# Weaving the high and low weights of a tile element by element, with activation rows 320 columns apart

## The chip, the cores and the metric

The kernel runs on one core of one Trainium2 chip. The metric is the device time of one execution, in microseconds (us). The kernel before takes 2366.43 us (median of three runs, 2366.19 to 2366.48). One more execution was taken with the hardware profiler; its own time is 2366.29 us, and the instructions in its trace span 2364.5 us of that.

## The reference, cut to what matters

A two-layer encoder on 256 tokens plus 16 meta tokens (272 rows, 256 in the last layer's later steps), width 2048, all in float32:

```python
proj = h @ w_in                       # (272 x 2048) @ (2048 x 6176): both head groups
y_gla = gla_mixer(...)                # bidirectional gated linear attention, 4 heads
y_na = na_mixer(...)                  # 2-D neighbourhood attention, 16 heads
mix = concat([y_gla, y_na]) @ w_out   # (272 x 2048) @ (2048 x 2048)
h = layer_norm(ALPHA * h + mix)
ff = square(relu(h @ w_ff1)) @ w_ff2  # 2048 -> 8192 -> 2048
h = layer_norm(ALPHA * h + ff)
```

Nearly all of the arithmetic is in the four products with `w_in`, `w_out`, `w_ff1` and `w_ff2`.

## The kernel before, in words

**Precision.** TensorE takes the operands as float32r, which keeps fewer bits than float32. So each number is split into a high part (rounded to float32r) and a low part (what the rounding lost), and a product is three matmuls: high weights by high activations, high weights by low activations, low weights by high activations.

**Weights.** They stream from HBM once, in 768 tiles of 128 partitions by 1024 columns (`order`, `weights`, `made`, lines 150 to 184). A tile is eight blocks of 128 x 128. For each, SP issues a DMA into `raw` (L179), ScalarE casts `raw` to `wh` (L180), VectorE subtracts, `wl = raw - wh` (L181). The pool `wst` has three buffers each of `raw`, `wh` and `wl`, so a tile's cast waits until the matmuls with the `wh` of three tiles before are done, and `weights` makes each tile one tile ahead of its use. The first tile is put together in smaller pieces (`head`, L186 to L202).

**Activations.** They lie transposed, 128 features by tokens, as a `Pair` (L43): one tile of `[128, 2, PITCH]` whose two rows are the high and the low part. With `PITCH` = 288 a row starts 1152 bytes behind the one before it. In this program the high rows of the tiles that the four products read start at multiples of 256 bytes in the partition, the low rows 128 bytes past such a multiple, and every block of `wh` and `wl` at a multiple of 512 bytes plus 256. In the last layer, where only 256 tokens are left, some pairs are dense: the low row follows at column 256.

**Products.** `by_m` (L250) makes one output block of 128 features at a time: for every weight tile `eight` (L204) issues its matmuls into one PSUM bank. Where 272 (or 258, 274) columns are wanted these are 16 matmuls with `wh` (L216: each block twice, with the high and the low row) and 8 with `wl` (L219). Where 256 are wanted (`once`) they are 8 matmuls of 512 columns with `wh` (L213: the high and the low row in one instruction) and 8 of 256 columns with `wl` (L219). `by_k` (L230) uses a tile for four outputs at once, 24 matmuls (L246); that is 56 of the 768 tiles, 16 of them with 256 columns. Every matmul loads its own weights: 128 columns of 4 bytes in each partition, read at a step of 4 bytes.

**Around them.** Attention, gates and norms are generators that `pump` steps between the products (queues `fg` and `bg`); `issue_after(self.wl)` puts what they issue behind the latest split of weights. A scheduler orders each engine's instructions by its own estimates. The matmuls of these parts, among them the low-rank gate (L403, loads of 64 and 32 columns) and `gla_head` (L446 to L642), use other tiles than `wh` and `wl`. `merge` (L543) and `gather` (L534) of `gla_head` work on strided rows. `mean` (L876) takes its pair, "sp", from `pair` (L277) too.

The constructor of the program in `kernel` sets a scratch of 8192 bytes in each partition for DMA descriptors.

Of the kernel before, what the change touches and what calls it, by code (L numbers as in the profile page):

```python
# [7 lines left out]
F32 = mybir.dt.float32  # L8
F32R = mybir.dt.float32r
U8 = mybir.dt.uint8  # L10
AF = mybir.ActivationFunctionType
ALU = mybir.AluOpType
PSUM = bass.MemoryType.PSUM

P = 128
# [4 lines left out]
L = T + NM  # L20
# [6 lines left out]
WB = 1024  # L27
# [9 lines left out]
WARM = 14  # L37
MEET = 2
PAD = 40
PITCH = 288  # L40


class Pair(tuple):  # L43
# [10 lines left out]
class Trunk:  # L54
# [117 lines left out]
    def made(self, ap, ends):  # L172
        if ap is None:
            return None
        nc = self.nc
        raw, wh, wl = (self.wp.tile([P, WB], d, name=nm, tag=nm)
                       for nm, d in (("raw", F32), ("wh", F32R), ("wl", F32R)))
        for c in map(slice, (0,) + ends, ends):
            nc.sync.dma_start(raw[:, c], ap[:, c])  # L179
            nc.scalar.copy(wh[:, c], raw[:, c])  # L180
            self.wl = nc.vector.tensor_tensor(wl[:, c], raw[:, c], wh[:, c].bitcast(F32), ALU.subtract).ins  # L181
        if not ends:
            self.head(ap, raw, wh, wl)
        return wh, wl

    def head(self, ap, raw, wh, wl):  # L186

        nc, q = self.nc, WB // 4
        both = self.xr.tile([P, 2, q + L], F32, name="head", tag="head", bufs=1)
        self.x[:2] = [self.pair(self.xp, "x", c) for c in range(2)]  # L190
        for c in range(2):
            nc.sync.dma_start(both[:, c], self.i["head"][:, c])
        nc.sync.dma_start(raw[:, 2 * q:], ap[:, 2 * q:])
        for c in range(2):
            at = slice(c * q, c * q + q)
            h, lo = (t[:, :L] for t in self.x[c])
            todo = [(both[:, c, q:], h, lo), (both[:, c, :q], wh[:, at], wl[:, at])]
            for args in todo[::-1] if c else todo:
                self.split(*args)
        for at in (slice(2 * q, 3 * q), slice(3 * q, WB)):  # L200
            nc.scalar.copy(wh[:, at], raw[:, at])
            self.wl = nc.vector.tensor_tensor(wl[:, at], raw[:, at], wh[:, at].bitcast(F32), ALU.subtract).ins  # L202

    def eight(self, ps, wh, wl, x, n, first, last, once):  # L204

        mm = self.nc.tensor.matmul
        c = lambda w, j: w[:, j * P:j * P + P]  # L210
        for j, v in enumerate(x):
            if once:
                mm(ps, lhsT=c(wh, j), rhs=v.once, start=first and not j, stop=False)  # L213
                continue
            for i in range(2):
                mm(ps[:, :n], lhsT=c(wh, j), rhs=v[i][:, :n], start=first and not i + j, stop=False)  # L216
        o = ps[:, T:] if once else ps[:, :n]
        for j, (h, _) in enumerate(x):
            mm(o, lhsT=c(wl, j), rhs=h[:, :T if once else n], start=False, stop=last and j == 7)  # L219
# [10 lines left out]
    def by_k(self, acts, n, before, wide=False):  # L230

        ps = [self.pm.tile([P, 512], F32, name="mm", tag="mm") for _ in range(4)]
        if wide:
            ps += [self.bank() for _ in range(4)]
        nk = len(acts)
        for k in range(0, nk, 2):
            before(k)
            for g in range(0, len(ps), 4):
                wh, wl = self.weights()
                parts = ((wh, 0), (wh, 1), (wl, 0))  # L240
                order = [(j, p, m) for j in range(2) for p in range(3) for m in range(4)]
                by_output = k == nk - 2 or k == 0 and not wide
                order.sort(key=lambda o: (o[0], o[2] // 2) if wide and not k + g else (by_output and o[2], o[1] // 2))
                for j, p, m in order:
                    c = j * 512 + m * P
                    self.nc.tensor.matmul(ps[g + m][:, :n], lhsT=parts[p][0][:, c:c + P], rhs=acts[k + j][parts[p][1]][:, :n],  # L246
                                          start=k + j + p == 0, stop=k == nk - 2 and j + p == 3)
        return [p[:, :n] for p in ps]

# [25 lines left out]
        self.nc.vector.tensor_tensor(dst[low:low + n], src, dst[high[0]:high[0] + n].bitcast(F32), ALU.subtract)  # L275

    def pair(self, pool, name, c):  # L277
        both = pool.tile([P, 2, PITCH], F32R, name=f"{name}{c}", tag=f"{name}{c}", bufs=1)
        return Pair(both, dense=name in ("y", "u") and not self.full)


# [92 lines left out]
    def load_gates(self):  # L374

        place = lambda c: self.yp.tile([P, 2, PITCH], F32, name=f"gw{c}", tag=f"y{c}", bufs=1).rearrange("p a c -> p (a c)")[:, :512]
        *self.wup, self.wlr = (place(c) for c in (8, 9, 10))
# [563 lines left out]
    def reuse(self, name, c, dtype):  # L941

        t = self.xp.tile([P, 2, PITCH], dtype, name=f"{name}{c}", tag=f"x{c}", bufs=1)
        return t.rearrange("p a c -> p (a c)")[:, :512]
# [235 lines left out]
```

## Time and profile before

| | |
|---|---|
| median of 3 runs | 2366.43 us |
| profiled execution, its own time | 2366.29 us |
| span of its instructions | 2364.5 us |
| granted TensorE clock, mean | 0.999 |
| HBM read | 414.03 MB, 176 GB/s over the span |
| share of 16 DMA engines used by the weights' queue | 55.8% |

How to read it: PE is TensorE's matmuls and PEld its weight loads, which overlap the matmuls; DVE is VectorE, ACT is ScalarE, POOL is GpSimd, SP is SyncE. A group's row gives line, engine, operation, out<-in, shape and count, then busy time, mean duration of one, and the idle time before. A matmul's duration is longer than its pace, since matmuls are pipelined: the mean 272-column matmul lasts 287 ns, but the next one starts about 125 ns after it. The pace is read from the chain of work that ended last, where the time of a piece is the time to the next piece, so that its time over its count is the spacing of its matmuls.

### The profile page before, as it was taken

Reading aid. Unit: us, or ns where it says so; the run is one execution under the profiler, and the core shown is the slowest. Engines: PE = TensorE matmul, PEld = TensorE weight load, DVE = VectorE, ACT = ScalarE, POOL = GpSimd, SP = SyncE. Lnnn points to the kernel's source line nnn. Section 1 sums busy time; section 2 is a strip of 40 time slices with the busy share of each in tenths; the row PEclk is TensorE's granted clock in tenths of the full one; section 3 lists DMA queues with packets and bytes.
Section 4 is the critical chain, followed back from the end, with each engine's and each line's share of the span. In section 5 each row is a group of like instructions: output and inputs, shape, how many; then the busy total and the mean of one; then the engine's idle time right before and its main releaser. Section 6 shows DMA issues by size and latency. Waiting matters only on the chain.

```text
span 2364.5 us, 44607 instructions
## 1 busy us (share of the span) xinstructions
PE 2356.2 (100%) x18180; PEld 2241.9 (95%) x18180; DVE 1520.8 (64%) x2432; ACT 1219.3 (52%) x2100; POOL 136.2 (6%) x200
## 2 busy tenths in 40 slices
PE   9999999999999999999999999999999999999998
PEld 9999999999999999999999899999988888888888
DVE  5588777775544455546576787778766455666654
ACT  5666664564433344444456666655644333444443
POOL 0021100100000000000030111101100000000000
PEclk9999999999999999999999999999999999999999
DMA  7454445555555555555555555455566666556664
GB/s 261 153 160 153 156 135 176 173 176 178 177 178 176 176 177 179 177 177 174 177 184 171 164 160 165 155 160 188 187 192 190 189 187 188 188 190 212 195 188 144
DMA packets 118301, 419.02 MB, mean 177 GB/s; under 512 B 13512, under 2 KB 14024, under 8 KB 118096
## 3 DMA queue, kind: packets, MB, share of 16 engines
q1 hardware_dynamic: 117808, 415.65, 55.8%
q8 instruction: 142, 2.33, 0.4%
q14 instruction: 63, 0.52, 0.1%
q10 hardware_dynamic: 288, 0.52, 0.1%
HBM read 414.03 MB, written 2.10 MB: 176 GB/s over the span
## 4 chain that ended last, share of the span: by engine, by line
PE 98%; DVE 1%; issue 0%; ACT 0%; POOL 0%; DVEq 0%; ACTq 0%; POOLq 0%
PE mm L216 35%; PE mm L219 29%; PE mm L213 22%; PE mm L246 6%; PE bg L246 1%; PE bg L757 1%; PE mm L696 1%; PE bg L557 0%; PE bg L403 0%; DVE wl L181 0%; PE mm L722 0%; PE mm L446 0%; PE bg L883 0%; PE bg L608 0%; PE bg L638 0%
## 5 line engine op out<-in xcount | busy, mean ns | idle before, releaser
L181 DVE TENSOR_TENSOR wl<-raw,wh 128x1024 fp32r<-128x1024 f32 (+1 forms) x768 | 941.8, 1227 | 621.5 <-ACT wh L180 618.4
L180 ACT CAST wh<-raw 128x1024 fp32r<-128x1024 f32 (+1 forms) x768 | 803.5, 1047 | 919.4 <-PE mm L216 367.7
L216 PE MATMUL mm<-x,wh 128*128 128x272 f32 (+2 forms) x4224 | 569.8, 287 | 0.0
L216 PEld LDWEIGHTS mm<-x,wh 128*128 128x128 f32 x4224 | 541.1, 188 | 0.8 <-PE mm L696 0.2
L219 PE MATMUL mm<-x,wl 128*128 128x272 f32 (+3 forms) x3264 | 466.9, 285 | 0.0
L219 PEld LDWEIGHTS mm<-x,wl 128*128 128x128 f32 x3264 | 437.5, 189 | 11.6
L213 PE MATMUL mm<-x,wh 128*128 128x512 f32 x1152 | 290.1, 394 | 0.0
L213 PEld LDWEIGHTS mm<-x,wh 128*128 128x128 f32 x1152 | 207.2, 189 | 37.9 <-PE mm L696 0.4
L219 PE MATMUL mm<-y,wl 128*128 128x272 f32 (+1 forms) x1408 | 200.5, 285 | 0.0
L219 PEld LDWEIGHTS mm<-y,wl 128*128 128x128 f32 x1408 | 189.5, 189 | 6.5
L216 PE MATMUL mm<-y,wh 128*128 128x272 f32 (+1 forms) x1440 | 193.3, 286 | 0.0
L216 PEld LDWEIGHTS mm<-y,wh 128*128 128x128 f32 x1440 | 184.3, 188 | 0.0
L213 PE MATMUL mm<-y,wh 128*128 128x512 f32 x688 | 172.6, 392 | 0.0
L219 PE MATMUL mm<-u,wl 128*128 128x272 f32 (+1 forms) x1024 | 145.8, 285 | 0.0
L213 PEld LDWEIGHTS mm<-y,wh 128*128 128x128 f32 x688 | 123.6, 189 | 21.9
L219 PEld LDWEIGHTS mm<-u,wl 128*128 128x128 f32 x1024 | 137.8, 189 | 4.8
L216 PE MATMUL mm<-u,wh 128*128 128x272 f32 (+1 forms) x1056 | 141.2, 286 | 0.0
L216 PEld LDWEIGHTS mm<-u,wh 128*128 128x128 f32 x1056 | 134.9, 188 | 0.0
L213 PE MATMUL mm<-u,wh 128*128 128x512 f32 x496 | 124.2, 392 | 0.0
L213 PEld LDWEIGHTS mm<-u,wh 128*128 128x128 f32 x496 | 89.2, 189 | 15.9
L246 PE MATMUL mm<-x,wh 128*128 128x272 f32 (+1 forms) x512 | 73.3, 288 | 0.0
L246 PEld LDWEIGHTS mm<-x,wh 128*128 128x128 f32 x512 | 67.9, 191 | 0.0
(273 smaller groups left out, 1856.5 us busy)
## 6 DMA issues: line engine op xcount, KB each, us to landing
raw<-in_wff SPq DMA_DIRECT2D x512, 512.0 KB, 3.6
raw<-in_win SPq DMA_DIRECT2D x190, 512.0 KB, 3.8
raw<-in_wout SPq DMA_DIRECT2D x64, 512.0 KB, 3.6
nb<-in_nab SPq DMA_DIRECT2D x16, 352.0 KB, 4.7
xraw<-in_xT SPq DMA_DIRECT2D x7, 272.0 KB, 5.2
out<-out SPq DMA_DIRECT2D x5, 256.0 KB, 3.2
brow<-in_norm SPq DMA_DIRECT2D x4, 256.0 KB, 4.8
gw<-in_wup SPq DMA_DIRECT2D x4, 196.0 KB
```

Of the source, the lines that this page charges most:

```text
L180: nc.scalar.copy(wh[:, c], raw[:, c])
L181: self.wl = nc.vector.tensor_tensor(wl[:, c], raw[:, c], wh[:, c].bitcast(F32), ALU.subtract).ins
L213: mm(ps, lhsT=c(wh, j), rhs=v.once, start=first and not j, stop=False)
L216: mm(ps[:, :n], lhsT=c(wh, j), rhs=v[i][:, :n], start=first and not i + j, stop=False)
L219: mm(o, lhsT=c(wl, j), rhs=h[:, :T if once else n], start=False, stop=last and j == 7)
L246: self.nc.tensor.matmul(ps[g + m][:, :n], lhsT=parts[p][0][:, c:c + P], rhs=acts[k + j][parts[p][1]][:, :n], start=k + j + p == 0, stop=k ...
L696: nc.tensor.matmul(ps[hh][:, t * NKEY:t * NKEY + NKEY], lhsT=q[hs, NM + t * P:NM + t * P + P], rhs=k[hs, t, :], start=True, stop=True)
L757: nc.tensor.matmul(po[t][hs, :P], lhsT=v2[ts, hs] if rest else v1[:, t, hs], rhs=p2[ts, hh, :] if rest else p1[:, 2 * hh + t, :], start=re ...
```

## The change

The two halves of a weight tile share one tile `w` of 2 x 1024 + 64 columns. High and low weights alternate: high, low, high, low. So one half's 128 columns of a block are read (and written, by the cast and the split) at a step of 8 bytes, and a block of one half covers 1024 bytes instead of 512. `BASE` puts the weave 32 columns (128 bytes) into the tile. In the changed program the high half of every block starts 128 bytes past a multiple of 256, the low half 132. `PITCH` becomes 320, so every row, high or low, of the pairs for the four products starts at a multiple of 256 bytes. The pair "sp" of `mean` gets rows of 272. There are still three buffers, now of `raw` and `w`. The scratch for descriptors becomes 2048 bytes, which makes room for the wider rows. Each engine issues as many instructions as before: the same matmuls with the same columns, casts, splits and DMAs. The scheduler places some of them a little differently; on PE that is a few dozen matmuls.

```diff
-PITCH = 288
+PITCH = 320
+BASE = 32
...
     def made(self, ap, ends):
...
-        raw, wh, wl = (self.wp.tile([P, WB], d, name=nm, tag=nm)
-                       for nm, d in (("raw", F32), ("wh", F32R), ("wl", F32R)))
+        raw = self.wp.tile([P, WB], F32, name="raw", tag="raw")
+        blocks = raw.rearrange("p (b c) -> p b c", c=P)
+        wh, wl = self.woven()
         for c in map(slice, (0,) + ends, ends):
             nc.sync.dma_start(raw[:, c], ap[:, c])
-            nc.scalar.copy(wh[:, c], raw[:, c])
-            self.wl = nc.vector.tensor_tensor(wl[:, c], raw[:, c], wh[:, c].bitcast(F32), ALU.subtract).ins
+            self.halves(blocks, wh, wl, slice(c.start // P, c.stop // P))
...
+    def woven(self):
+        flat = self.wp.tile([P, 2 * WB + 64], F32R, name="w", tag="w")
+        both = flat[:, BASE:BASE + 2 * WB].rearrange("p (b c i) -> p i b c", c=P, i=2)
+        return both[:, 0], both[:, 1]
+
+    def halves(self, raw, wh, wl, at):
+        self.nc.scalar.copy(wh[:, at], raw[:, at])
+        self.wl = self.nc.vector.tensor_tensor(wl[:, at], raw[:, at], wh[:, at].bitcast(F32), ALU.subtract).ins
...
     def eight(self, ps, wh, wl, x, n, first, last, once):
...
-        c = lambda w, j: w[:, j * P:j * P + P]
+        c = lambda w, j: w[:, j]
...
     def by_k(self, acts, n, before, wide=False):
...
-                    c = j * 512 + m * P
-                    self.nc.tensor.matmul(ps[g + m][:, :n], lhsT=parts[p][0][:, c:c + P], rhs=acts[k + j][parts[p][1]][:, :n],
+                    self.nc.tensor.matmul(ps[g + m][:, :n], lhsT=parts[p][0][:, 4 * j + m], rhs=acts[k + j][parts[p][1]][:, :n],
...
     def pair(self, pool, name, c):
-        both = pool.tile([P, 2, PITCH], F32R, name=f"{name}{c}", tag=f"{name}{c}", bufs=1)
+        both = pool.tile([P, 2, L if name == "sp" else PITCH], F32R, name=f"{name}{c}", tag=f"{name}{c}", bufs=1)
...
-    nc = bacc.Bacc("TRN2", target_bir_lowering=False, num_devices=1, dynamic_dma_scratch_size=8192)
+    nc = bacc.Bacc("TRN2", target_bir_lowering=False, num_devices=1, dynamic_dma_scratch_size=2048)
```

`head` is changed in the same way: it splits its pieces by blocks, through `halves`.

More of the change, by code (lines that the diff above doesn't have):

```diff
@@ L175, in made, with head @@
         nc = self.nc
-        raw, wh, wl = (self.wp.tile([P, WB], d, name=nm, tag=nm)
-                       for nm, d in (("raw", F32), ("wh", F32R), ("wl", F32R)))
+        raw = self.wp.tile([P, WB], F32, name="raw", tag="raw")
+        blocks = raw.rearrange("p (b c) -> p b c", c=P)
+        wh, wl = self.woven()
         for c in map(slice, (0,) + ends, ends):
             nc.sync.dma_start(raw[:, c], ap[:, c])
-            nc.scalar.copy(wh[:, c], raw[:, c])
-            self.wl = nc.vector.tensor_tensor(wl[:, c], raw[:, c], wh[:, c].bitcast(F32), ALU.subtract).ins
+            self.halves(blocks, wh, wl, slice(c.start // P, c.stop // P))
         if not ends:
-            self.head(ap, raw, wh, wl)
+            self.head(ap, raw, blocks, wh, wl)
         return wh, wl
-    def head(self, ap, raw, wh, wl):
+    def woven(self):
[5 more added lines that the diff above has]
+        self.wl = self.nc.vector.tensor_tensor(wl[:, at], raw[:, at], wh[:, at].bitcast(F32), ALU.subtract).ins
+    def head(self, ap, raw, blocks, wh, wl):
         nc, q = self.nc, WB // 4
@@ L194, in head @@
         for c in range(2):
-            at = slice(c * q, c * q + q)
+            at = slice(2 * c, 2 * c + 2)
             h, lo = (t[:, :L] for t in self.x[c])
-            todo = [(both[:, c, q:], h, lo), (both[:, c, :q], wh[:, at], wl[:, at])]
+            todo = [(both[:, c, q:], h, lo), (both[:, c, :q].rearrange("p (b c) -> p b c", c=P), wh[:, at], wl[:, at])]
             for args in todo[::-1] if c else todo:
                 self.split(*args)
-        for at in (slice(2 * q, 3 * q), slice(3 * q, WB)):
-            nc.scalar.copy(wh[:, at], raw[:, at])
-            self.wl = nc.vector.tensor_tensor(wl[:, at], raw[:, at], wh[:, at].bitcast(F32), ALU.subtract).ins
+        for at in (slice(4, 6), slice(6, 8)):
+            self.halves(blocks, wh, wl, at)
     def eight(self, ps, wh, wl, x, n, first, last, once):
         mm = self.nc.tensor.matmul
-        c = lambda w, j: w[:, j * P:j * P + P]
+        c = lambda w, j: w[:, j]
         for j, v in enumerate(x):
```

## The prediction

> **What bounds the kernel now.** I read the head of the page first, for the busy shares and the clock, then the chain that ended last.
>
> ```profile
> span 2364.5 us, 44607 instructions
> PE 2356.2 (100%) x18180; PEld 2241.9 (95%) x18180; DVE 1520.8 (64%) x2432; ACT 1219.3 (52%) x2100; POOL 136.2 (6%) x200
> PEclk9999999999999999999999999999999999999999
> ## 4 chain that ended last, share of the span: by engine, by line
> PE 98%; DVE 1%; issue 0%; ACT 0%; POOL 0%; DVEq 0%; ACTq 0%; POOLq 0%
> PE mm L216 35%; PE mm L219 29%; PE mm L213 22%; PE mm L246 6%; PE bg L246 1%; PE bg L757 1%; PE mm L696 1%; PE bg L557 0%; PE bg L403 0%; DVE wl L181 0%; PE mm L722 0%; PE mm L446 0%; PE bg L883 0%; PE bg L608 0%; PE bg L638 0%
> ```
>
> TensorE is never idle, its clock is granted in full, and 98% of the chain is its own matmuls, nearly all on weight tiles (L213, L216, L219, L246). Nothing outside TensorE is worth saving. What counts is the spacing of matmuls, and how often each occurs. Counts come from the groups:
>
> ```profile
> L181 DVE TENSOR_TENSOR wl<-raw,wh 128x1024 fp32r<-128x1024 f32 (+1 forms) x768 | 941.8, 1227 | 621.5 <-ACT wh L180 618.4
> L180 ACT CAST wh<-raw 128x1024 fp32r<-128x1024 f32 (+1 forms) x768 | 803.5, 1047 | 919.4 <-PE mm L216 367.7
> L216 PE MATMUL mm<-x,wh 128*128 128x272 f32 (+2 forms) x4224 | 569.8, 287 | 0.0
> L213 PE MATMUL mm<-x,wh 128*128 128x512 f32 x1152 | 290.1, 394 | 0.0
> L216 PE MATMUL mm<-y,wh 128*128 128x272 f32 (+1 forms) x1440 | 193.3, 286 | 0.0
> L213 PE MATMUL mm<-y,wh 128*128 128x512 f32 x688 | 172.6, 392 | 0.0
> L216 PE MATMUL mm<-u,wh 128*128 128x272 f32 (+1 forms) x1056 | 141.2, 286 | 0.0
> L213 PE MATMUL mm<-u,wh 128*128 128x512 f32 x496 | 124.2, 392 | 0.0
> ```
>
> L216 has 6720 matmuls, 16 to a tile: 420 narrow tiles. L213 has 2336, 8 to a tile: 292 wide tiles. There are 768 tiles, so 56 are left for L246, of which 40 have 272 columns and 16 have 256 (the loops say so). The spacings are in the chain in order of time, here from a narrow stretch, a wide one, and the two stretches of L246:
>
> ```profile
> 970.89 1.98 PE mm L216 x16
> 972.87 1.00 PE mm L219 x8
> ...
> 1998.85 1.84 PE mm L213 x8
> 2000.69 0.95 PE mm L219 x8
> ...
> 493.82 24.10 PE mm L246 x192
> 1679.72 23.04 PE mm L246 x192
> ```
>
> Over their counts: 272 columns every 123.8 ns with `wh` and 125.0 with `wl`; 512 columns every 230; 256 columns every 118.8; in L246 125.5 (272) and 120.0 (256). A narrow tile takes 2.98 us, a wide one 2.79. Check: 420 x 2.98 + 292 x 2.79 + 40 x 24 x 0.1255 + 16 x 24 x 0.120 = 1251.6 + 814.7 + 120.5 + 46.1 = 2233 us, 94% of the span. So **one per cent on these spacings is 22 us**.
>
> **What is in a spacing.** Three rows tell of it: loads of several widths, and two pieces of plain float32 matmuls that stream 128 columns.
>
> ```profile
> L216 PEld LDWEIGHTS mm<-x,wh 128*128 128x128 f32 x4224 | 541.1, 188 | 0.8 <-PE mm L696 0.2
> L403 PEld LDWEIGHTS bg<-x,ws 128*64 128x64 f32 x32 | 4.3, 135 | 0.5
> L403 PEld LDWEIGHTS bg<-x,ws 128*32 128x32 f32 x32 | 3.5, 108 | 0.0
> ...
> 135.85 0.45 PE bg L612 x4
> ...
> 223.26 0.22 PE bg L718 x2
> ...
> 56.66 3.99 PE bg L403 x32
> ```
>
> From 32 to 128 columns a load grows by 80 ns, 0.83 ns a column: 128 columns are read in about 107 ns, so a load runs under nearly all of a 272-column stream. L612 loads 128 columns each time as well, and gives 112 ns (0.45 / 4) for 128 float32 columns; L718 gives 110. A float32 column passes at about half the pace, so I take 112 ns as the price of 256 float32r columns, 0.4375 ns each: the load is the same, but the row is read at half the rate. By that price 272 columns are worth 119.0 ns, 512 are worth 224.0, and the spacings above have 4.8 to 6.8 ns more. My reading: while a load reads 4 bytes per 0.83 ns, the row is read at 4 bytes per 0.44 ns; the two walk through the partition at different speeds, and some of the steps meet and cost time. With a step of 8 bytes both walk at about the same speed, and with all rows at one phase (mod 256 bytes) and the weights 128 bytes off it, they keep their distance.
>
> L403 speaks against this reading. Its loads are 64 and 32 columns, yet its 272-column matmuls come every 124.7 ns (3.99 / 32). If loads were the whole cause, they would be faster. So the surplus may belong to the start of each matmul, and weaving would then find nothing.
>
> **The change part by part.**
>
> *Matmul spacing.* I take the price of L612 (112 ns), the nearest row, since it has full loads running alongside. Ends: L718's 110 ns below; above, a surplus that doubles (both under the rivals). Narrow tile: 24 x 119.0 = 2.856, saves 0.124 x 420 = 52 us. Wide tile: 8 x 224 + 8 x 112 = 2.688, saves 0.102 x 292 = 30 us. L246: 960 x 6.5 ns + 384 x 8.0 ns = 9 us. **Sum -91 us.** If only half of the surplus goes: -46.
>
> *Loads.* As many as before. Their reads now touch twice the span of bytes. Decisive is whether 0.83 ns a column holds: from 0.95 on, 128 columns take 122 ns and loads set the pace of narrow tiles. [...]
>
> *Cast and split.* Now at a step of 8 bytes. Rows for strided work of these engines:
>
> ```profile
> L543 DVE TENSOR_TENSOR S<-S,dec 128x272 f32<-128x272 f32 x64 | 27.1, 449 | 0.8 <-ACT U L534 0.5
> L910 DVE TENSOR_TENSOR s<-s,acc 128x272 f32<-128x272 f32 x28 | 12.2, 435 | 0.0
> ...
> L534 ACT COPY U<-S x104: 388/414/549, 111.4 to 1480.5; 128x272 f32<-128x272 f32 x56, 128x256 f32<-128x256 f32 x48
> ...
> ACT wh L180 <- PE mm L216: 367.7, 216, 2.1
> ```
>
> VectorE's strided `merge` (L543; a step of 8 bytes at its first level) takes 449 ns, 14 more than contiguous L910: for 1024 elements at most 53 ns. ScalarE's slowest `gather` takes 549 ns against a median of 414, 135 ns for 272 elements, so a cast costs at most 508 ns more, 1.56 us; the lower end is no difference. For the end of the kernel I take 0 either way: a tile lasts 2.8 to 3.0 us, and 1.56 (ACT) and 1.28 us (DVE) fit into it beside the other work (ACT at worst 1219 + 768 x 0.508 = 1609 us, 68%; DVE 66%).
>
> *One tile for both halves.* The cast, which now often waits for L216's matmuls (last row), must wait for those with `wl` too, 1.0 us later. Behind it in ACT's queue stand evictions and the split on DVE; all of it may start up to 1 us later. What hides that is depth: with three buffers a tile freed at the end of its matmuls is wanted after two more tiles, 5.6 to 6 us later, and cast plus split take 2.3 us (2.9 at worst). If that cover went, each tile would lose the missing part. SP's DMA into `raw` waits for the split as before. At the very start, where the chain shows DVE's L181, PE may wait for whole blocks: under 2 us. Scratch and "sp" are worth nothing: the weights' DMAs come from SP, and `mean` is 36 matmuls.
>
> The profiled execution is 2366.3 us, 0.1 below the median, with 1.8 us around its span. **2366.3 - 91 = 2275 us.**
>
> **The rivals.**
>
> *All of the surplus goes.* L718's 110 ns (0.43 a column): narrow tile 24 x 116.9 = 2.806, -73; wide 8 x 220 + 8 x 110 = 2.640, -44; L246 -12. Time 2237. For it: reads at one speed and a fixed distance could leave nothing to meet. Against: L718's row is two matmuls, and at half the rate. [...]
>
> *The change does nothing to the pace.* The surplus is the matmul's own, whatever the load reads, as L403's 124.7 ns suggest. Then nothing in the chain moves but what alignment of the low rows gives or takes, half a per cent: 2366, 2355 to 2378. Against: L612's matmuls have loads and starts as well, and carry less. [...]
>
> *Locked in step the wrong way (slower).* At equal speeds, whatever distance the two reads start with stays for the whole load. If 128 bytes is a bad distance, every step meets, where now only some do. I price it as the surplus once more, since the load runs under nearly all of a narrow stream and now at twice the bytes: +91, 2457 us. It decides if the phase of weights against rows (128 bytes of 256) is one that collides. For it: the surplus is real and the profile shows no such phase. Against: a fixed distance can as well be one at which nothing meets.
>
> *Loads become the bound (slower, a tail).* If a load column takes 25% longer, 1.04 ns, a load is 133 ns plus the 5 ns that L612 has over 107: 138. Narrow tiles +139 us (24 x 13.8 ns x 420), wide ones +45 (8 x 19.2 x 292), L246 +19: 2569. For it: the bytes spanned double. [...]
>
> **How the numbers follow.** Forecast (2245 to 2330, from nearly all of the surplus to somewhat under half) 0.45; all of it (2205 to 2245) 0.18; nothing (2355 to 2378) 0.12; wrong step (2378 to 2520) 0.19; loads 0.06. "Nothing" splits into 0.04 faster, 0.05 same, 0.03 slower; same is within 0.2%, 4.7 us, about what a measurement can tell. Faster: 0.45 + 0.18 + 0.04 = 0.67. Same: 0.05. Slower: 0.28. The range runs from 2205, which leaves 0.03 out, to 2430, which leaves out the loads and over half of the wrong step, some 0.16. The likeliest case's own range is 2245 to 2330.
>
> **What would show it.** Right: in the chain a narrow tile near 2.86 us and a wide one near 2.69, the spacing with `wh` and with `wl` alike (all rows have one phase), PEld still at 188 ns, ACT and DVE still waiting for PE. "All" would show 2.81 and 2.64. "Nothing" keeps 2.98 and 2.79. The wrong step shows narrow spacings near 129 with loads of 188; loads as the bound show PEld above 188 and 256- and 272-column matmuls at one spacing. Casts over 1.5 us, or PE idle before L216 with ACT or DVE as releaser, would mean that the cover went. The forecast is wrong if the surplus is no meeting of two reads, as L403 hints.

## The result and the profile after

The changed kernel takes **2384.81 us** (median of four runs, 2383.56 to 2386.72), the one before 2366.31 beside it (2365.74 to 2366.48): a ratio of 1.0079, 95% interval 1.0063 to 1.0095. It is 18.5 us slower. The forecast was 2275 us, faster by 91. The profiled execution of the changed kernel takes 2384.99 us.

The head of the page of the changed kernel, its chain, and the groups that answer to those of before:

```profile
span 2383.2 us, 44639 instructions
...
PE 2372.5 (100%) x18180; PEld 2270.6 (95%) x18180; DVE 1537.2 (65%) x2432; ACT 1275.1 (54%) x2100; POOL 118.5 (5%) x200
...
PEclk9999999999999999999999999999999999999999
...
PE 95%; DMA 2%; DVE 1%; ACT 1%; issue 1%; POOL 0%; SPq 0%; DVEq 0%; ACTq 0%; POOLq 0%
...
L195 DVE TENSOR_TENSOR w<-raw,w 128x1024 fp32r<-128x1024 f32 (+1 forms) x770 | 943.1, 1225 | 617.9 <-ACT w L194 609.6
L194 ACT CAST w<-raw 128x1024 fp32r<-128x1024 f32 (+1 forms) x770 | 871.7, 1133 | 722.3 <-PE mm L229 523.2
L226 PE MATMUL mm<-x,w 128*128 128x272 f32 (+2 forms) x4224 | 574.9, 289 | 0.2 <-ACT w L194 0.2
L226 PEld LDWEIGHTS mm<-x,w 128*128 128x128 f32 x4224 | 547.1, 196 | 1.3 <-ACT w L194 0.6
```

L226, L229, L223 and L255 are the matmuls that were L216, L219, L213 and L246. TensorE is as busy as before and its clock is granted in full (0.999 on the mean, as before), so nearly all of the added time must lie in the spacing of the matmuls again. A load lasts 196 ns and not 188. A cast lasts 1133 ns and not 1047; a split has not changed (1225, 1227). ScalarE is still at 54%. The chain, though, has lost 3% to DMA, ACT and DVE, which it hardly held before. All of that lies in two stretches, the first 37 us and from 1223 to 1298 us. At a wait of TensorE the chain goes on to what was waited for, and through the work ahead of that, while TensorE itself was busy; how long TensorE stood still is in the waits below.

The chain of the changed kernel in order of time (start, duration, piece, count): a narrow stretch near 384 us, another near 970 us, a wide one near 2000 us, and between them the long pieces by k:

```profile
384.01 2.03 PE mm L226 x16
386.04 1.01 PE mm L229 x8
...
500.54 23.91 PE mm L255 x192
...
972.45 1.99 PE mm L226 x16
974.44 0.99 PE mm L229 x8
...
1692.12 23.05 PE mm L255 x192
...
1999.99 1.85 PE mm L223 x8
2001.84 0.97 PE mm L229 x8
```

A narrow tile takes 2.98 us in one place and 3.04 in another. From the starts of the matmuls, counting the tiles with another tile right behind them: of those with 272 columns, 285 took 2.98 us before and none 3.04; now 256 take 2.99 and 43 take 3.04, over half of these in one stretch (377 to 450 us). A wide tile takes 2.82 us and not 2.79. The long pieces by k have not lost.

From the starts of the matmuls in the two traces, first to last, the span has grown from 2356.8 to 2375.6 us, by 18.8. The spacings hold +14.2 of it:

| matmuls | mean spacing before, ns | after | sum, us |
|---|---|---|---|
| 272 columns, high weights | 123.9 | 125.0 | +6.5 |
| 272 columns, low weights | 125.0 | 124.8 | -1.0 |
| 512 columns | 230.5 | 231.3 | +2.1 |
| 256 columns, low weights | 119.0 | 121.2 | +5.0 |
| 258 and 274 columns, by k, the rest | | | +1.6 |

The remaining 4.6 us is time in which TensorE stood still. The waits of TensorE in the changed kernel name a part of it:

```profile
PE mm L255 <- ACT w L194: 1.0, 1, 1.0
PE mm L255 <- ACT x L277: 0.9, 1, 0.9
PE bg L617 <- DVE y L278: 0.5, 1, 0.5
PE mm L223 <- ACT ft L442: 0.4, 1, 0.4
```

With two smaller ones (0.3 and 0.2) that is 3.3 us, against 1.0 before, beside a first wait of 1.2 us that both have. So 2.3 of the 4.6 us are named.

### The profile page after: what moved, and what is told of

The parts are those of the page before. It is cut to its first block, busy times and chain, and to the rows that moved or that the text cites. A ratio compares the mean times of both kernels' runs of the same rounds, so it can differ in the third digit from the quotient of the medians.

```text
span 2383.2 us, 44639 instructions
## 1 busy us (share of the span) xinstructions
PE 2372.5 (100%) x18180; PEld 2270.6 (95%) x18180; DVE 1537.2 (65%) x2432; ACT 1275.1 (54%) x2100; POOL 118.5 (5%) x200
## 4 chain that ended last, share of the span: by engine, by line
PE 95%; DMA 2%; DVE 1%; ACT 1%; issue 1%; POOL 0%; SPq 0%; DVEq 0%; ACTq 0%; POOLq 0%
PE mm L226 35%; PE mm L229 29%; PE mm L223 22%; PE mm L255 4%; DMA raw<-in_win 1%; ACT w L194 1%; PE bg L766 1%; DVE w L195 0%; PE mm L705 0%; PE bg L566 0%; PE bg L255 0%; PE bg L412 0%; DVE acc L994 0%; DMA xraw<-in_xT 0%; PE mm L731 0%
## 5 line engine op out<-in xcount | busy, mean ns | idle before, releaser
L195 DVE TENSOR_TENSOR w<-raw,w 128x1024 fp32r<-128x1024 f32 (+1 forms) x770 | 943.1, 1225 | 617.9 <-ACT w L194 609.6
L194 ACT CAST w<-raw 128x1024 fp32r<-128x1024 f32 (+1 forms) x770 | 871.7, 1133 | 722.3 <-PE mm L229 523.2
L226 PE MATMUL mm<-x,w 128*128 128x272 f32 (+2 forms) x4224 | 574.9, 289 | 0.2 <-ACT w L194 0.2
L226 PEld LDWEIGHTS mm<-x,w 128*128 128x128 f32 x4224 | 547.1, 196 | 1.3 <-ACT w L194 0.6
L229 PE MATMUL mm<-x,w 128*128 128x272 f32 (+3 forms) x3264 | 469.9, 287 | 0.0
L229 PEld LDWEIGHTS mm<-x,w 128*128 128x128 f32 x3264 | 443.5, 196 | 10.2
L223 PE MATMUL mm<-x,w 128*128 128x512 f32 x1152 | 290.9, 394 | 0.4 <-ACT ft L442 0.4
L223 PEld LDWEIGHTS mm<-x,w 128*128 128x128 f32 x1152 | 214.4, 195 | 32.6 <-ACT ft L442 0.6
L229 PE MATMUL mm<-y,w 128*128 128x272 f32 (+1 forms) x1408 | 202.5, 286 | 0.0
L229 PEld LDWEIGHTS mm<-y,w 128*128 128x128 f32 x1408 | 192.6, 195 | 6.0
L226 PE MATMUL mm<-y,w 128*128 128x272 f32 (+1 forms) x1440 | 195.0, 288 | 0.0
L226 PEld LDWEIGHTS mm<-y,w 128*128 128x128 f32 x1440 | 186.5, 195 | 0.0
L223 PE MATMUL mm<-y,w 128*128 128x512 f32 x688 | 173.2, 393 | 0.0
L229 PE MATMUL mm<-u,w 128*128 128x272 f32 (+1 forms) x1024 | 146.6, 286 | 0.0
L223 PEld LDWEIGHTS mm<-y,w 128*128 128x128 f32 x688 | 128.0, 195 | 18.8
L229 PEld LDWEIGHTS mm<-u,w 128*128 128x128 f32 x1024 | 139.6, 196 | 4.4
L226 PE MATMUL mm<-u,w 128*128 128x272 f32 (+1 forms) x1056 | 142.1, 288 | 0.0
L226 PEld LDWEIGHTS mm<-u,w 128*128 128x128 f32 x1056 | 136.1, 196 | 0.0
L223 PE MATMUL mm<-u,w 128*128 128x512 f32 x496 | 124.7, 393 | 0.0
L223 PEld LDWEIGHTS mm<-u,w 128*128 128x128 f32 x496 | 92.3, 195 | 13.6
L255 PE MATMUL mm<-x,w 128*128 128x272 f32 (+1 forms) x768 | 98.0, 288 | 2.2 <-ACT w L194 1.0
L255 PEld LDWEIGHTS mm<-x,w 128*128 128x128 f32 x768 | 96.2, 195 | 3.2 <-ACT w L194 1.5
```

The source lines that it names most:

```text
L194: self.nc.scalar.copy(wh[:, at], raw[:, at])
L195: self.wl = self.nc.vector.tensor_tensor(wl[:, at], raw[:, at], wh[:, at].bitcast(F32), ALU.subtract).ins
```

## The experiments

**What is in a spacing: matmuls alone.** These kernels leave the whole computation out. Each has pieces of 64 matmuls on zeros, one source line per piece, with one thing varied at a time:

```python
for i in range(64):
    nc.tensor.matmul(ps[:cols, :n], lhsT=W[:, phase + i % 8 * 128 * step:...:step], rhs=X[:, i % 4 * 512:i % 4 * 512 + n], ...)
```

> Leaves out the whole computation: 61 pieces of 64 matmuls each on zeros, one source line per piece, so that each gives a mean spacing. Varied one at a time: the phase and the step (4, 8, 12, 16 bytes) of the weights that a load reads, the number of weight columns loaded (128, 64, 32, 16), the phase of the row, the number of columns streamed, and the number format. Theory M (the load's reads and the row's reads meet, my prediction's): at 272 columns with step 4 near 124 ns, narrower loads fall towards 119, step 8 differs by phase, some phases near 119 and others near 130. Theory S (the surplus belongs to the start of each matmul): 124 to 125 ns at 272 columns for every phase, step and width of load, and the same 5 to 7 ns above 0.4375 ns a column at 128, 256 and 512 columns. Theory R (spacing is rounded up to a grid): the sweep from 256 to 304 columns rises in stairs and not in a line.

In the chain of this kernel a piece's time over its count is its spacing. A piece of bfloat16 at 272 columns (L188), and two of plain float32 at 128 columns, where each matmul has two records, with loads of 128 columns (L200) and of 32 (L203):

```profile
512.47 7.43 PE mm L188 x64
...
548.11 14.29 PE mm L200 x128
562.40 14.09 PE mm L203 x128
```

That is 116 ns for bfloat16, and 112 and 110 ns a record for float32. The float32r pieces at 272 columns lie between 122 and 128 ns at steps of 4 and 8 bytes (means over the piece, from the matmuls' starts) and do not fall with the load: at one phase 125.4 ns with 128 weight columns, 124.1 with 64, 126.7 with 32 and 124.5 with 16 (with 128 always the same block). But they do differ by the phase of the weights: 123.3 ns with the weights 64 bytes on, 126.7 at 128. My forecast's theory falls by the first, theory S by the second, and the stairs of theory R did not show: 120.0 at 256 columns, 120.8 at 258, 129.8 at 274, 131.6 at 288, 137.7 at 304 rise unevenly, without steps of 16.

> Leaves out the whole computation: pieces of 64 matmuls on zeros from 208 to 512 columns, each in three forms: loads of 16 columns with a normal row, loads of 128 columns with the row read at one repeated address, and both normal; then whole tiles of the kernels' layouts, twice each. If load and row reads meet, a normal row with a 16-column load is as fast as a repeated address at every width. If the row's own read has a cost of its own, the surplus over 0.4375 ns a column stays with the 16-column load at widths that are no multiple of 256 and goes only with the repeated address. The tiles: both passes within 5 ns of each other, and the layout of before at 2970 to 2990 ns narrow and 2793 to 2807 wide.

Here every width runs in three forms: loads of 16 columns (the first of each three rows), the row read at one repeated address (the second), and both normal (the third). The rows are 208 columns (normal only), 256 and 272:

```profile
47.28 7.15 PE mm L34 x64
...
96.48 7.47 PE mm L55 x64
103.95 7.17 PE mm L58 x64
111.12 7.67 PE mm L61 x64
...
164.06 7.97 PE mm L82 x64
172.03 7.59 PE mm L85 x64
179.63 8.02 PE mm L88 x64
```

At 208 columns the spacing is 111.7 ns, as it is at 128, 192, 224 and 240: at none of these widths did a load of 128 columns follow another sooner. At 256 columns: 116.7 with the small load, 112.0 with the repeated address, 119.9 normal. At 272: 124.5, 118.6, 125.3. So **at 272 columns 5.9 of the 6.7 ns over the repeated address stay when the load shrinks to an eighth: they are the row's own reading**. At 256 the load has 3 ns in it, and twice that in the run below. So theory S, though it has no place for the phase, is right on most of the size at 272 columns, and a meeting of load and row plays a part at 256.

> Leaves out the whole computation: pieces of 64 matmuls each on zeros. First, the same 272-column piece after four different predecessors. Theory A (spacing is set by the addresses: phase of row against phase of weights modulo 256 bytes, and step): the repeats agree within 0.3 ns, about 125.7 at phase 0, 123.3 with the weights 64 bytes on. Theory H (a cycle is locked in by what ran before): repeats differ by 1 to 5 ns. Second, what the surplus is. If the load makes it, 256 and 512 columns fall to 112 and 224 ns with loads of 16 columns; if it is the float32r row's, they stay at 118 to 120 and 227 to 235, a row read at one repeated address changes it, and bfloat16 stays at 0.4167 ns a column plus 2.5 at all sizes. Third, the floor of a load: 128 columns streamed show 111.7 ns at step 4; at step 8, 112 if such a load costs no more, 118 to 120 if the 8 ns by which loads took longer in the changed kernel are real.

The same 272-column piece after four predecessors gave 125.4, 125.4, 125.3 and 125.3 ns, and with the weights 64 bytes on 123.3 and 123.4: theory A here. With loads of 64 to 16 columns, 256 columns came down to 113.3 ns (116.7 in the run above, with the same addresses) and 512 did not (230 to 232). bfloat16, by the pieces of the chain, took 56.1 ns at 128 columns, 82.5 at 192, 109.2 at 256, 115.8 at 272, 129.2 at 304, 169.2 at 400 and 215.8 at 512: all within 0.3 ns of 0.4167 ns a column plus 2.5. The floor of a load, in the chain and in the groups of loads: 128 columns streamed with weights at a step of 4 (L31) and of 8 bytes (L70):

```profile
33.55 7.09 PE mm L31 x64
...
154.78 7.49 PE mm L70 x64
```

```profile
L70 PEld LDWEIGHTS mm<-X,W 128*128 128x128 f32 x64 | 7.7, 196 | 0.2
...
L31 PEld LDWEIGHTS mm<-X,W 128*128 128x128 f32 x64 | 7.2, 192 | 0.0
```

The piece with a step of 16 bytes lies in a stretch of this run in which the granted clock was 0.50 (166 to 193 us). So that step is read from the first of these kernels, where the clock was 1.0 and 272 columns were streamed:

```profile
200.59 14.94 PE mm L98 x64
```

Within the piece, from the starts, 111.7 ns at a step of 4 and 117.8 at 8; 233 at 16. **A load at a step of 8 bytes takes 6 ns longer to get out of the way of the next.** That is 5%; at a step of 16 bytes the time doubles.

**Each part of the change alone.** Only the wider rows, with the weights in two tiles as before (the rows of "sp" and the scratch are those of the changed kernel):

```diff
-PITCH = 288
+PITCH = 320
```

> Only the wider rows: activations 320 columns apart, weights in two tiles, unwoven, step 4 bytes. Theory P (the phase of the rows makes the loss: with all rows at one phase of 256 bytes the high and low rows no longer alternate): about 2380 us, 272-column spacings with high weights up from 123.9 to near 125. Theory W (the weave makes the loss): 2366 us within 2, spacings as before. My prediction's meeting of reads: within 10 us of before, since the two reads still walk at different speeds.

2383.61 us, ratio 1.0071 (1.0056 to 1.0086). This part alone costs 17 us, nearly as much as the whole change. In its chain a narrow tile takes 3.04 us:

```profile
975.78 2.03 PE mm L216 x16
977.81 1.01 PE mm L219 x8
```

The 272-column spacing with high weights rose from 123.9 to 126.1 ns (+13.2 us in sum), with low weights from 125.0 to 126.1 (+3.0); nothing else moved by 1 us. Theory P holds for this half.

Only the weave, with `PITCH` back at 288 in the changed kernel:

> Only the weave: step 8 bytes in one tile, but activations 288 columns apart as before, so the rows of low halves are 128 bytes off those of high halves. Theory W (the weave makes the loss): about 2385 us, loads near 196 ns, 256-column spacings at 121. Theory P (the rows' phase does): near 2366, 272-column spacing with high weights near 124 and alternating. Theory M: the half of the matmuls whose row is 128 bytes off has another spacing than the other half.

2387.50 us, ratio 1.0090 (1.0073 to 1.0107): 21 us. So both theories were true by their own runs, and the two losses don't add: 17 and 21 make 18.5 together. A cost for each part is not what happens. What counts is the layout as a whole.

High and low weights in one tile, not woven, rows 320 apart:

```diff
-        both = flat[:, BASE:BASE + 2 * WB].rearrange("p (b c i) -> p i b c", c=P, i=2)
+        both = flat[:, BASE:BASE + 2 * WB].rearrange("p (i b c) -> p i b c", c=P, i=2)
```

> High and low weights in one tile, but not woven: high blocks, then low blocks, step 4 bytes; rows 320 apart. Theory T (the shared tile costs: the cast waits for the last matmul of the tile): about 2385 us, or at least the 5 us of idle time beyond the spacings. Theory W (the step of 8 bytes costs): same time as with the wider rows alone, loads back at 188 ns, casts back at 1048 ns.

2393.88 us, ratio 1.0115 (1.0100 to 1.0130): slower than the woven one, with loads back at 188 ns. Neither theory had that. This layout has the weights 128 bytes past the rows' phase at a step of 4 bytes, and so the next runs took the layouts one by one.

**The layouts alone.** Whole narrow and wide tiles in the kernel's order, without the rest of the kernel.

> Leaves out the whole computation: whole narrow and wide tiles on zeros, in the kernel's order, 5 of each layout. Varied: how far apart the rows of the two halves are (256, 272, 288, 304, 320 columns), the phase of the weights in steps of 16 or 32 bytes, the step (4 or 8 bytes). Theory A (addresses alone set the spacings): the four layouts that ran as kernels come out as there: rows 288 apart, phase 0, step 4: 124.3 ns over a narrow tile; rows 320, phase 0, step 4: 126.1; rows 320, phase 128, step 4: 126.7; rows 320, phase 128, step 8: 124.9; rows 288, phase 128, step 8: 125.4; and one layout should be better than all, near 123.3 (weights 64 bytes on). Theory C (the losses come from the casts' and evictions' traffic beside the matmuls): these layouts agree within 0.3 ns here, where no other engine runs.

104 layouts, five tiles of each. Four of the five layouts that had run as kernels came out as theory A said, within 0.8 ns; the fifth, that of before, was the first piece, which holds the slow start of the kernel. So the run of micro4 has the kernels' layouts once more, twice each and alike to 5 ns. From its chain, five tiles to a piece. Narrow: rows 288 apart with weights at 0 (L236), rows 320 apart with weights at 0 (L255), at 64 (L267), at 128 (L279), and woven at 128 (L310). Wide: dense rows with weights at 0 (L250), rows 320 apart with weights at 64 (L274):

```profile
577.85 14.91 PE mm L236 x120
...
606.79 13.97 PE mm L250 x80
620.76 15.04 PE mm L255 x120
...
649.76 14.80 PE mm L267 x120
664.56 13.88 PE mm L274 x80
678.45 15.20 PE mm L279 x120
...
750.97 14.94 PE mm L310 x120
```

A tile, without the edges of a piece: 2.980 us (L236, the 2.98 of the kernel before), 3.008 (L255), 2.960 (L267), 3.040 (L279), 2.987 (L310); wide 2.793 (L250) and 2.773 (L274). No cast and no eviction runs beside these tiles, so **the addresses alone make these differences**.

**Back in the kernel.** The best layout of the sweep is unwoven, with rows 320 apart and the weights 64 bytes on. The kernel is that of the wider rows alone, with 64 bytes put ahead of the weights' pool and 192 behind it:

```diff
+SHIFT = 16
...
+        pool("s1", bufs=1).tile([P, SHIFT], F32, name="s1", tag="s1")
         self.wp = pool("wst", bufs=3)
+        pool("s2", bufs=1).tile([P, 64 - SHIFT], F32, name="s2", tag="s2")
```

> Rows 320 apart, weights in two tiles, unwoven (step 4), all weights 64 bytes further on. Theory A (the phase of the weights against the rows, and the step, set the spacing): from the pieces that ran alone, 2960 ns for a narrow tile (2983 before), 2773 for a wide one (2796 before), 123.3 ns in the pieces by k: 420 x -23 + 292 x -23 + 960 x -2.3 ns = -18.6 us, about 2348, faster than both. Theory W (only the weave matters): about 2366. Theory P (one phase for all rows makes the loss by itself): about 2383, as with the wider rows alone.

**2347.89 us, ratio 0.9922 (0.9907 to 0.9936)**: faster than both kernels, and where the pieces put it. A narrow and a wide tile of its chain:

```profile
975.79 1.97 PE mm L219 x16
977.76 0.99 PE mm L222 x8
...
1993.54 0.91 PE mm L222 x8
1994.45 1.86 PE mm L216 x8
```

2.96 and 2.77 us. With one phase for all rows, and moving the weights by 64 bytes only, 36 us separate this kernel from that of the wider rows alone.

The same with `SHIFT = 32`, which is the layout of the one unwoven tile, in two tiles:

> The same with the weights 128 bytes further on: step 4, two tiles, the addresses modulo 256 of the run with one unwoven tile. Theory A: same time as that run within 3 us, about 2393. Theory T (sharing one tile costs the cast a wait that reaches TensorE): 5 us or more below it, at 2384 to 2388.

2392.95 us, ratio 1.0111 (1.0096 to 1.0126), 0.9 below the run with one tile. Theory A again. The difference is within the noise of the two ratios. The waits of TensorE on the work around the weights, first with one tile, then with two:

```profile
PE mm L255 <- ACT w L194: 0.9, 1, 0.9
```

```profile
PE mm L249 <- DVE x L272: 0.2, 1, 0.2
```

With one tile TensorE waits once for a cast of weights, 0.9 us, and with two not at all. The changed kernel has the same wait (1.0 us, above), but the weave alone, which shares a tile too, has only one of 0.2 us. So the wait doesn't come with every shared tile, and about 1 us is the most that it cost.

The changed kernel with `BASE = 16`, its weave 64 bytes in:

> The changed kernel, woven, rows 320 apart, but the tile starts 64 bytes in and not 128 (BASE 16). Theory A: from the pieces that ran alone a narrow tile takes 3067 ns against 2987, a wide one 2804 against 2820: 420 x 80 - 292 x 16 ns = +29 us, about 2414. Theory L (a load at a step of 8 bytes costs the same wherever it starts, and that is the loss): 2385, no change.

2399.92 us (2394.80 to 2401.54), ratio 1.0143 (1.0126 to 1.0160): slower still, by the phase alone, so theory L falls. The size is off: +15 and not +29. In the profiled execution 292 narrow tiles take 3.04 us and only 12 take 3.067, the value that had been measured alone. That execution is the shortest of the four (2394.80 us); the other three are 5 to 7 us longer, and no trace shows whether more of their tiles took 3.067.

**The finest sweep, and a miss.** Unwoven, rows 320 apart, the weights in steps of 4 bytes:

> Leaves out the whole computation: narrow and wide tiles on zeros, rows 320 apart, step 4, the weights moved on by 0 to 252 bytes in steps of 4. Theory A in its narrow form (the spacing is set by which addresses meet, modulo 256): narrow tiles from 2960 to 3040 ns with no value far below 2960, since even 16-column loads left 124.4 ns at 272 columns; 256-column matmuls with the low weights at 113.3 to 114.0 ns near phase 64 only, and 512-column ones at 227 to 234. If the row's own reading is not the floor, some phase between the 16-byte steps gives 272 columns at 119 ns, a tile of 2860.

No narrow tile of the 64 phases was under 2960 ns; 10 reached it, so 123.3 ns is the floor of 272 columns with full loads in these layouts. The pieces with small loads had said nearly the same (122.2 ns at the least). For wide tiles 28 bytes looked best: 2747 ns. So the next kernel takes 28 bytes for tiles with wide products and 64 for the others:

```diff
+        at, self.count = 7 if KINDS[self.count] == "W" else 16, self.count + 1
+        wh, wl = (self.wp.tile([P, WB + 64], F32R, name=nm, tag=nm)[:, at:at + WB] for nm in ("wh", "wl"))
```

> Rows 320 apart, unwoven, and the phase of the weights chosen per tile: 64 bytes on for tiles used by narrow products, 28 bytes on for tiles used by wide ones. Theory A: from the pieces that ran alone a wide tile takes 2747 ns at 28 bytes against 2774 at 64: 292 x -27 ns = -7.9 us from the 2347.9 of 64 bytes for all, about 2340; spacings 226.8 and 116.6 in the wide tiles, 123.3 in the narrow ones. Theory N (such a value of a single phase does not survive beside the casts and evictions of a whole kernel): 2348 or above.

2354.49 us, ratio 0.9950 (0.9936 to 0.9963): 6.6 us worse than one phase of 64 bytes, not 8 better. Its wide tiles in the chain:

```profile
1990.11 1.87 PE mm L216 x8
1991.97 0.93 PE mm L222 x8
```

2.80 us. The low weights are at 116.7 ns as expected, the 512-column matmuls at 233.1 and not 226.8. But this holds for 258 of the wide tiles that have another tile right behind them. Ten others take the 2.747 us of the piece that ran alone, five of them on end:

```profile
1349.57 1.81 PE mm L216 x8
1351.38 0.93 PE mm L222 x8
```

In these ten the 512-column matmuls follow each other after 227, 227 and 226 ns over and over, as in the piece alone; in the 258 they alternate between 231 and 236. So the value does survive beside casts and evictions, but rarely. The last run looked at what the layout does alone after other predecessors:

> Leaves out the whole computation: 5 tiles on zeros of each of six layouts, each six times, after 1 or 2 tiles of another layout. Theory B (a layout can have more than one steady cycle, and what ran before chooses): the wide tile with the weights 28 bytes on shows 512-column spacings of 226.8 after some predecessors and 233 after others, the woven narrow tile at 64 bytes 3040 and 3067 ns, the narrow tile at phase 0 125.3 and 126.1 ns; the narrow tile at 64 bytes stays at 2960. Theory C (traffic of other engines moves the cycle in the whole kernel): each layout gives one value after all six predecessors, 226.8 for the wide tile at 28 bytes.

In its chain: the wide tile with the weights 28 bytes on (L43), and the changed kernel's own narrow layout, woven at 128 bytes, after wide tiles at 0 (L395) and after wide tiles at 192 (L417); five tiles each:

```profile
38.68 14.03 PE mm L43 x80
...
620.86 15.21 PE mm L395 x120
...
662.78 14.94 PE mm L417 x120
```

The wide layout gives 2.800 us after all six predecessors, as in most of the kernel, with the same 231 and 236 ns in turn. So theory N, which blamed the casts and evictions, isn't needed. (The tiles that ran ahead of the 2.747 us in the finest sweep, with the weights 24 bytes on, are not among the six, and there the first of the four tiles still took 2.81 us.) The changed kernel's layout holds 3.040 us for all five tiles after two of the predecessors and 2.987 after four; woven at 64 bytes, 3.067 after four and 3.040 after two. **So a layout can have more than one steady cycle.** Once in one, tiles stay in it: in the changed kernel no narrow tile passes from 2.99 to 3.04 us or back right behind another. That what ran before chooses the cycle, and not chance, is likely but not shown: each predecessor ran once here, though in the run of micro4 the changed kernel's layout came twice after the same one, both times at 2.987. 2.987 and 3.040 us are the two values of the changed kernel's chain (2.99 for 256 tiles, 3.04 for 43), here with no cast or eviction beside them. Mixed in this share they make +14 us by the sum below, near the +12.6 that the four widths of the table above hold together. The layout of the wider rows alone gave 3.008 after all six; in its kernel 88 tiles take 3.01 and 191 take 3.04, so there either a further predecessor or the other engines' work plays a part. The runs don't tell which.

All layouts together. "Worked out" is 420 times the narrow difference to before plus 292 times the wide one, from the tiles alone (two values where there are two cycles):

| rows apart, weights' step and phase | narrow alone, us | wide alone | worked out, us | measured, us |
|---|---|---|---|---|
| 288, 4, 0 (before) | 2.980 | 2.793 | | |
| 320, 4, 0 (wider rows alone) | 3.008 | 2.793 | +12 | +17.0 |
| 288, 8, 128 (weave alone) | 3.008 | 2.820 | +20 | +20.9 |
| 320, 8, 128 (the change) | 2.987 or 3.040 | 2.820 | +11 or +33 | +18.5 |
| 320, 4, 128 (two tiles) | 3.040 | 2.805 | +29 | +26.6 |
| 320, 8, 64 (`BASE` 16) | 3.040 or 3.067 | 2.803 | +28 or +39 | +33.5 |
| 320, 4, 64 | 2.960 | 2.773 | -14 | -18.5 |
| 320, 4, 64 and 28 | 2.960 | 2.747 or 2.800 | -22 or -6 | -11.8 |

In the last two rows the pieces by k save about 4.3 us more each (in the first of them 272 columns go from 125.4 to 123.4 ns, 256 columns from 119.9 to 113.7).

## Why the prediction was wrong

**The step that failed is the price and the cause of the surplus** ("I take 112 ns as the price of 256 float32r columns", and "the two walk through the partition at different speeds, and some of the steps meet and cost time"). L612's 112 ns is the floor of back-to-back loads: float32r at 208 columns has the same 111.7 ns, and plain float32 falls to 110 with loads of 32 columns. It is the price of a load, and doesn't say what a float32r row costs. (That a float32 column passes at about half the pace does hold: 256 of them took 217 ns a record in the first run of pieces, against 120.0 in float32r.) That 256 float32r columns read at one repeated address take 112.0 ns as well is luck; as the row lies they take 116.7 or 113.3 with the smallest load. A row of 272 columns needs 118.6 ns only when it reads one address over and over; read as it lies it takes 124.5 ns with the smallest load and, with full loads, no less than 123.3 at any of the 64 phases. So of the 124.3 ns there was about 1 ns to win, not 5. The sums built on the price are right; the price isn't. The forecast summed -91 us on the spacings; the runs show +14.2 for the change and -18 for the best layout found. The forecast itself named the row that spoke against it, L403 with loads of 64 and 32 columns at 124.7 ns, and gave the case 0.12. The pieces with loads of 16 columns are that row made into an experiment.

**The bound** was read rightly: before and after, all but a few us is in the spacings of four lines, and one per cent on them is 22 us.

**The loads** did not stay at 188 ns, as the sum took them, and no run shows that at a step of 8 bytes they could: they took 196, and their floor rose from 111.7 to 117.8 ns. That may be what 256 columns show, which went from 119.0 to 121.2 ns (+5.0 us): in the pieces alone they come every 120.0 ns at all four phases of a step of 8, not far above the floor, where 272 columns are long enough to hide it. But that the load sets the 121.2 is not shown. The rival with loads as the bound asked for 25%; the runs show 5%.

**The phase** was bounded by a rival ("locked in step the wrong way"), at +91. Its kind was right: at a fixed step the phase of weights against rows decides (3.040 against 2.960 us a tile by 64 bytes alone, unwoven). Its size was the whole surplus once more. Between these two phases it is 80 ns of a narrow tile's 2980, 34 us over 420 tiles; the worst of the 64 phases alone, 108 bytes, took 3.11 us, 62 us over 420 tiles more than the best. The measured 2384.8 us lies in that rival's range (2378 to 2520), and so in the prediction's whole range of 2205 to 2430, but by luck: the rival's signs were narrow spacings near 129 ns and loads of 188, and the runs show 125.0 and 196. And the alignment of the low rows, which the rival "nothing" held to half a per cent, costs 17.0 us (0.7%) by itself. The phase of the weave was not even unlucky: 128 bytes gave the shortest narrow tile of the eight phases tried at a step of 8 with rows 320 apart, when it was in its shorter cycle.

**Cast, split, shared tile**: right in kind. The cast takes 86 ns more, the split nothing, and neither sets the end. The shared tile lets the cast wait for L229 (523 us in all, off the path) and reaches TensorE twice, for 1.0 and 0.2 us; with 0.9 us between the runs with one and with two tiles, it was not worth a term. Of TensorE's other 3.4 us of standstill the waits name 1.1 more than before; the rest is not explained.

**Format and phase.** bfloat16 takes 115.8 ns at 272 columns, on the straight line of its other widths; float32r takes 125.3. And the weights' phase reaches the rows: with the rows 320 apart, moving the weights by 64 bytes and nothing else took the 256-column matmuls from 119 ns (8 in 0.95 us, the wider rows alone) to 113.7 (8 in 0.91).

**What stays open**: why reading distinct addresses costs a float32r row 5 to 6 ns, what picks the cycle of a layout that has two, and 2.3 us of standstill.

## What to carry to other kernels

Before a surplus is called removable, measure its floor: shrink the suspect to an eighth (here the load) and see whether the surplus shrinks. Where thousands of equal matmuls follow each other, the phase of the weights against the rows, over 256 bytes, is worth a sweep of tiles alone; here it gave 0.8% for a shift of 64 bytes and forecast that kernel's time within 1 us. For two layouts with two cycles the forecast missed by about 14 us. So trust a layout of such a sweep only if it gives the same value after several predecessors.

## What the runs showed of the hardware that was not expected

- The spacing of these float32r matmuls is not a number but a cycle that repeats over a few matmuls, set by step and phase: 272 columns gave means from 122.2 to 129.5 ns with the same shape. A tile of 3.040 us, for one, is 127, 127 and 126 ns over and over. Some layouts have two cycles, and stay in one for many tiles (22 on end at 3.04 us in the changed kernel).
- 128-column float32r loads followed each other after 111.7 ns at a step of 4 bytes, 117.8 at 8 and 233 at 16.
- bfloat16 shows none of this in the few pieces that ran, all at one phase: 115.8 ns at 272 columns, with loads of 128 or of 32 columns, and with weights at a step of 2 or of 4 bytes.
